# Gate and up of a SwiGLU network by seven block products in place of eight, with spills through DRAM

## The chip, the cores and the metric

The kernel runs on one core of a Trainium2 chip. Times are device microseconds of one execution. The version before was run three times: 1843.7 to 1844.92 us, median 1844.18. A separate profiled execution gives the trace that is read here. Engines go by the names of the profile: PE (TensorE, matrix products), DVE (VectorE), ACT (ScalarE), POOL (GpSimd), SP (SyncE, which here only issues DMA transfers). POOL issues DMA transfers as well.

## The reference

A decoder trunk of two layers on x of 1024 tokens by D = 1024 features, with a conditioning vector c. Each layer is a token mixer and a feed-forward network (FFN), each behind an RMSNorm, an affine step from c, and a gated residual add:

```python
def swiglu_ffn(h, w_gate, w_up, w_down):
    return (jax.nn.silu(h @ w_gate) * (h @ w_up)) @ w_down
```

The FFN has F = 2816 hidden columns, 22 tiles of 128. The mixer of layer 0 is a causal convolution module (pointwise to 2D, a gate, 31 taps per channel, LayerNorm, silu, pointwise to D). The mixer of layer 1 takes trailing means over 2, 4, 8 and 16 tokens, less the token itself, and maps them by four small matrices. A last RMSNorm ends the stack. All is float32.

## The kernel before

Features lie on the 128 partitions (eight tiles k or d of 128), tokens on the free axis, in two chunks A and B of 512. So one matmul is a 128 x 128 weight tile by 128 x 512 activations into one PSUM bank. There are six banks for products and two spare ones. Every product is made of three matmuls (`products`, L434): weight and activation are each split into a rounded part and the rest, and high by high, high by low, and low by high are summed. The activations are `hhi` and `hlo`, the weights a pair in one `w` tile.

`load_weight` (L419) makes a `w` tile of 128 x 1024: SP loads `raw`, ACT casts it into the high half and writes its negative into the low half, and POOL issues a second, accumulating load of the same weights onto it (`summed`). The other way, a subtraction on DVE or POOL (`either` picks by a table of prices), is used for a few.

The order on PE is the order of the program: a list of units, each with the weights that it takes, which `run_units` (L561) loads up to five tiles ahead. Work for the other engines that may run beside them (taps of the convolution, norms, pooling) is cut into tasks that `pace` steps forward between products by the price table; `need` finishes a task. Each engine keeps its own row of instructions in order, and a waiting row holds back all behind it.

`ffn` (L921) goes through one chunk's 22 tiles: `ffn_p1` (L883) makes gate and up of a tile, 24 matmuls each, and g = silu(gate) x up as a pair (ACT, DVE, ACT, then DVE or POOL); `ffn_p2` (L909) multiplies two g's by their rows of the down weights into eight tiles d, and DVE adds each, scaled, to x. The whole of x and both chunks' g stay in SBUF. The main order (L1173 to L1224) is: FFN of A in layer 0 with B's taps beside it; B's convolution output and norm three units before its end; FFN of B with A's pooling beside it; FFN of A in layer 1, with the last down units of B and B's pooling; FFN of B. So while one chunk's norm is under way on DVE, PE has products of the other chunk.

Of the kernel before, what the change touches and what calls it, by code (L numbers as in the profile page):

```python
# [9 lines left out]
F32 = mybir.dt.float32  # L10
# [6 lines left out]
P = 128  # L17
D = 1024
# [18 lines left out]
GROUP = 2  # L37
# [12 lines left out]
OUT_B = 3  # L50
LOAD = {"load": 4.0, "slow": 18.0, "next": 4.0, "dots": 4.0}
# [67 lines left out]
def trunk(ctx, tc, xT, c, vec, ada, adan, w1f, w1, wdg, w2, wgu, wdn, wpl, out):  # L119
# [12 lines left out]
    def matmul(out, lhsT, rhs, start, stop):  # L132
        n = out.shape[-1]
        clock["PE"] += n / 2400 * (1 if rhs.dtype == F32R else 4) + 0.0025
        last_mm[0] = nc.tensor.matmul(out, lhsT, rhs, start=start, stop=stop).ins.name  # L135
# [27 lines left out]
    slots = ctx.enter_context(tc.tile_pool(name="slots", bufs=2 * KT))  # L163
# [3 lines left out]
    ps = ctx.enter_context(tc.tile_pool(name="ps", bufs=BANKS, space=bass.MemoryType.PSUM))  # L167

# [74 lines left out]
    def slot(ch, name, dt=F32R):  # L243

        return slots.tile([P, ch.n], dt, tag=f"s{ch.i}", name=nm(name))
# [10 lines left out]

    def gslots(ch):

        pair = wpair(ch, "g", F32R)
        return pair[:, 0, : ch.n], pair[:, 1, WSLOT - ch.n :]  # L260
# [30 lines left out]
    xp = [[cst.tile([P, 2, ch.n], F32, name=f"x_{ch.i}_{k}") for k in range(KT // 2)] for ch in chunks]  # L291
    x = [[pairs[k // 2][:, k % 2] for k in range(KT)] for pairs in xp]
    for k in range(KT // 2):
        load_next(xp[0][k], xT[0, :, 2 * k : 2 * k + 2])
# [139 lines left out]
    def products(out, wt, k, act, first, last, o=0, n=None):  # L434

        wk = slice(k * P, (k + 1) * P)
        for i, (wp, a) in enumerate(((0, 0), (0, 1), (1, 0))):
            cols = act[a][:, o : o + n] if n else act[a]
            matmul(out, wt[:, wp, wk], cols, start=first and i == 0, stop=last and i == 2)
# [104 lines left out]
    def norm(ch, l, ffn, key, keep=False, squares=None):  # L544
        h = [(slot(ch, "hhi"), slot(ch, "hlo")) for _ in range(KT)]
# [15 lines left out]
    def run_units(cap, early):  # L561

        queue = [w for ws, _ in units for w in ws]
        loaded = list(early)
        del queue[: len(early)]
        used = [0]

        def ahead(free):
            while queue and len(loaded) + used[0] - free < cap:
                src = queue.pop(0)  # L570
                loaded.append(src() if callable(src) else load_weight(src, summed=True))
                if len(loaded) > 1:
                    break

        for ws, emit in units:
            def take():
                ahead(0)
                used[0] += 1
                return loaded.pop(0)
            emit(take)  # L580
            used[0] -= len(ws)
            ahead(0)
            pace()
# [58 lines left out]
    def split_u(p):  # L642

        u = st["u", 0, p][:, HALO - 2 : HALO - 2 + A.n]
        hi, lo = st["us", p] = [slot(A, name) for name in ("uhi", "ulo")]
        S_.copy(hi, u)
        either(A.n).tensor_tensor(lo, u, hi.bitcast(F32), op=SUB)
# [101 lines left out]
    def layer_norm_silu(ch):  # L749
# [26 lines left out]
        hv = [(slot(ch, "vhi"), slot(ch, "vlo")) for _ in range(KT)]  # L776
# [60 lines left out]
    def pool_mixed(ch, k):  # L837
# [20 lines left out]
        hi, lo = st["mx", ch.i, k] = slot(ch, "mxhi"), slot(ch, "mxlo")  # L858
# [4 lines left out]
    def pool_out(ch, l, pair):  # L863
        def emit(take):
            wt = take()
            for gi in range(2):
                g = pair * 2 + gi
                for m in range(2):
# [4 lines left out]
                    update(ch, d, b, gate_m, l)  # L873
                pace()
# [8 lines left out]
    def ffn_p1(ch, l, f, pick, first):  # L883
        def emit(take):
            h = st["h", ch.i]
            outs = [output(name, pick) for name in ("gate", "up")]
            if first:
                wts = [take(), take()]
                for k in range(KT):
                    for o, wt in zip(outs, wts):  # L890
                        products(o, wt, k, h[k], k == 0, k == KT - 1)
                    pace()
            else:
                for o in outs:
                    wt = take()
                    for k in range(KT):
                        products(o, wt, k, h[k], k == 0, k == KT - 1)
                        if k % 4 == 3:
                            pace()
            hi, lo = st["g", ch.i, f] = gslots(ch)  # L900

            t = window(ch.n, "gt") if ch.i == 0 and l == 0 and f >= NF - 2 else temp(ch.n)
            S_.activation(t, outs[0], AF.Silu)
            V_.tensor_tensor(t, t, outs[1], op=MUL)
            S_.copy(hi, t)
            either(ch.n).tensor_tensor(lo, t, hi.bitcast(F32), op=SUB)
        return emit, (wgu[l, f, 0], wgu[l, f, 1])

    def ffn_p2(ch, l, fs, pick):  # L909
        def emit(take):  # L910
            wd = [take() for _ in fs]
            gs = [st.pop(("g", ch.i, f)) for f in fs]
            for d in range(KT):
                b = output("dn", pick)
                for i, (g, wt) in enumerate(zip(gs, wd)):
                    products(b, wt, d, g, i == 0, i == len(gs) - 1)
                update(ch, d, b, gate_f, l)
                pace()
        return emit, tuple(wdn[l, f] for f in fs)

    def ffn(ch, l, pick, at_end=False):  # L921

        us, pend = [], None
        ends = [NF - n for n in range(0, NF, GROUP)][::-1]
        if NF % GROUP == 1:
            ends[0] += 1
        for f0, f1 in zip([0] + ends, ends):
            fs = list(range(f0, f1))
            for i, f in enumerate(fs):
                us.append(ffn_p1(ch, l, f, pick, l == 0 and f == 0))  # L930
                if i == (len(fs) - 1 if fs[-1] == NF - 1 else 0) and pend is not None:
                    us.append(pend)
            last = at_end and fs[-1] == NF - 1
            pend = ending(ch, l, fs) if last else ffn_p2(ch, l, fs, pick)
        us.append(pend)
        return us

    def ending(ch, l, fs):
# [27 lines left out]
        def emit(take):  # L966
            wd = [take() for _ in fs]
            gs = [st.pop(("g", ch.i, f)) for f in fs]
# [81 lines left out]
    h_a = st["h", 0] = [(slot(A, "hhi"), slot(A, "hlo")) for _ in range(KT)]  # L1050
# [100 lines left out]
    unit(lambda take: T.__setitem__("ada_f", ada_task(0, (4, 5), "dots", "slow")))  # L1151
    for p in rest[len(rest) - HOLD - HOLD_LN : len(rest) - HOLD]:
        conv_in((B, p))
    need("ln_a")
# [9 lines left out]
    for p in rest[len(rest) - HOLD :]:  # L1164
        conv_in((B, p))
    need("norm_a")
# [6 lines left out]
    taps(B, *range(KT))  # L1173
    put("ln_b", lambda: layer_norm_silu(B))
    fa = ffn(A, 0, False)
    for i, (e, ws) in enumerate(fa):
        if i == GROUP + 1:
            unit(lambda take: finish(T["ada_f"]))
            unit(lambda take: T.__setitem__(("ada", 1), ada_task(1, range(6))))
        if i == len(fa) - OUT_B:  # L1180
            need("ln_b")
            sq_b = Squares(B)
            conv_out(B, sq_b)
            unit(lambda take: T.__setitem__("norm_bf", Task(norm(B, 0, True, ("h", 1), squares=sq_b), True)))
        unit(e, *ws)
    need("norm_bf")
    unit(lambda take: stretch.__setitem__(0, 1.0))

# [6 lines left out]

    unit(lambda take: (lax.__setitem__(0, True), st.__setitem__("taps_done", True)))

    def with_pool(us, ch, at, out_at):

        for i, (e, ws) in enumerate(us):  # L1200
            if i == at:
                if ch.i == 0:
                    ada_need((1, 0), (1, 1), (1, 2))
                put(("pool", ch.i), lambda: pool(ch))
            if i == out_at:
                need(("pool", ch.i))
                for q in range(2):
                    pool_out(ch, 1, q)
                if ch.i == 0:
                    ada_need((1, 3), (1, 4), (1, 5))  # L1210
                put(("nf", ch.i), lambda: norm(ch, 1, True, ("hn", ch.i), True))
            unit(e, *ws)
        need(("nf", ch.i))
        unit(lambda take: st.__setitem__(("h", ch.i), st["hn", ch.i]))


    fb_, fa_, last = ffn(B, 0, True), ffn(A, 1, True), ffn(B, 1, True, at_end=True)
    with_pool(fb_[:-1], A, 3, 14)
    with_pool(fa_[:1] + fb_[-1:] + fa_[1:-1], B, 5, 17)
    for i, (e, ws) in enumerate(last[:1] + fa_[-1:] + last[1:]):  # L1220
        if i == 3:
            put("final_a", lambda: final(A))
        unit(e, *ws)
# [53 lines left out]
```

## Time and profile before

| what | value |
|---|---|
| median of three runs | 1844.18 us |
| span of the profiled execution | 1848.1 us |
| PE busy | 1805.3 us, 8106 matmuls |
| DVE, ACT, POOL busy | 985.4, 971.0, 622.3 us |
| DMA | 388.61 MB, mean 210 GB/s |
| granted PE clock in the FFN stages | 0.99 to 1.00 |

The page gives busy time by engine, then 40 slices of the span, DMA queues, the chain of work that ended last, and groups of instructions. A group's row reads: line, engine, operation, output<-inputs by the program's names (buffer numbers left out), shapes, count, then busy time, mean ns of one, and idle time of its engine just before with what ended it. L113 and L135 are the two helpers that record every operation, so the tiles' names tell them apart. A waits row reads: total us, times, longest. A timeline row reads: start, length, engine. DMA rows end with the median us from issue to landing.

### The profile page before, as it was taken

To read this page: it belongs to the slowest core of one execution; us is meant where nothing else is said; L and a number is where in the kernel's file an instruction comes from. 1 tells how busy PE (TensorE), PEld (TensorE's weight loads), DVE (VectorE), ACT (ScalarE), POOL (GpSimd) and SP (SyncE) were. 2 spreads that over 40 slices of the span, in tenths; PEclk is the share of its full clock that TensorE was granted. 3 is DMA by queue.
4 is the path that set the end of the run, shared out by engine and by line. 5 is a ranking of instruction groups with operands and counts; after the bars stand their busy time and mean duration, and the time that the engine had idled before them with its cause. 6 is when DMAs were issued, how large, how long until landed. Compare 5 with 4: busy or idle time off the path is not lost.

```text
span 1848.1 us, 21822 instructions
## 1 busy us (share of the span) xinstructions
PE 1805.3 (98%) x8106; PEld 1483.8 (80%) x8106; DVE 985.4 (53%) x1522; ACT 971.0 (53%) x1244; POOL 622.3 (34%) x662
## 2 busy tenths in 40 slices
PE   6999999999999999999999999999999999999997
PEld 4777787888888888778888888888888888888886
DVE  7889857988884245576622233734432233323225
ACT  3666666767756364454544435644544454444443
POOL 3587534887834112263111112511111111111111
PEclk9999999999999999999999999999999999999998
DMA  6959888988978888989887888878878879788782
GB/s 262 292 159 236 202 237 246 255 212 217 237 194 224 220 221 199 278 257 268 229 199 176 211 182 201 186 180 211 190 173 207 198 178 247 176 208 195 181 197 69
DMA packets 108573, 388.61 MB, mean 210 GB/s; under 512 B 11825, under 2 KB 14001, under 8 KB 108466
## 3 DMA queue, kind: packets, MB, share of 16 engines
q0 software_dynamic: 44352, 161.50, 47.6%
q1 hardware_dynamic: 63024, 224.65, 35.0%
q8 instruction: 64, 1.05, 0.2%
q10 hardware_dynamic: 1090, 1.05, 0.2%
q14 instruction: 43, 0.35, 0.1%
HBM read 382.96 MB, written 4.19 MB: 209 GB/s over the span
## 4 chain that ended last, share of the span: by engine, by line
PE 84%; DVE 10%; DMA 4%; issue 1%; ACT 0%; SPq 0%; DVEq 0%
PE gate L135 24%; PE up L135 24%; PE dn L135 24%; PE y L135 6%; DVE ca L113 4%; DMA adaw<-in_ada_dram 3%; PE first L135 2%; PE a L135 2%; PE g L135 2%; DVE acc L113 1%; DVE adaw L113 1%; DVE t L113 1%; DVE hlo L113 1%; DVE x L113 1%; DMA adaw<-in_adan_dram 1%
## 5 line engine op out<-in xcount | busy, mean ns | idle before, releaser
L113 ACT CAST w<-raw 128x1024 fp32r<-128x1024 f32 x318 | 332.4, 1045 | 496.4 <-issue 286.5
L135 PE MATMUL dn<-g,w 128*128 128x512 f32 (+1 forms) x2160 | 490.5, 386 | 0.7 <-DVE t L113 0.7
L135 PEld LDWEIGHTS dn<-g,w 128*128 128x128 f32 x2160 | 399.7, 189 | 82.5 <-DVE t L113 1.5
L135 PE MATMUL gate<-hhi,w 128*128 128x512 f32 x1408 | 451.5, 390 | 1.9 <-DVE x L113 1.9
L135 PE MATMUL up<-hhi,w 128*128 128x512 f32 x1408 | 451.0, 390 | 0.0
L428 POOL DMA_DIRECT2D w<-in_wgu_dram x176 | 154.3, 877 | 744.0 <-ACT w L113 733.0
L113 ACT ACTIVATE w<-raw 128x1024 fp32r<-128x1024 f32 x308 | 325.2, 1056 | 0.0
L113 DVE SCALAR_TENSOR_TENSOR x<-dn,gains,x 128x512 f32<-128x512 f32 (+1 forms) x360 | 261.7, 735 | 110.7 <-PE dn L135 107.5
L135 PEld LDWEIGHTS gate<-hhi,w 128*128 128x128 f32 x1408 | 265.0, 188 | 57.4 <-DVE x L113 2.3
L113 DVE TENSOR_TENSOR t<-t,up 128x512 f32<-128x512 f32 x86 | 59.0, 686 | 469.7 <-PE up L135 447.4
L135 PEld LDWEIGHTS up<-hhi,w 128*128 128x128 f32 x1408 | 264.4, 188 | 54.7
L135 PE MATMUL gate<-hlo,w 128*128 128x512 f32 x704 | 274.8, 390 | 2.7 <-DVE hlo L113 2.7
L135 PE MATMUL up<-hlo,w 128*128 128x512 f32 x704 | 273.9, 389 | 0.0
L113 POOL TENSOR_TENSOR pa<-pa,pr 128x512 f32<-128x512 f32 x158 | 227.2, 1546 | 18.5 <-ACT pr L113 15.8
L113 DVE SCALAR_TENSOR_TENSOR ca<-u,vecs,ca 128x512 f32<-128x512 f32 x247 | 171.2, 746 | 0.2
L135 PEld LDWEIGHTS gate<-hlo,w 128*128 128x128 f32 x704 | 132.6, 188 | 31.4 <-DVE hlo L113 4.0
L135 PEld LDWEIGHTS up<-hlo,w 128*128 128x128 f32 x704 | 132.2, 188 | 27.1
L428 POOL DMA_DIRECT2D w<-in_wdn_dram x88 | 78.5, 892 | 217.3 <-ACT w L113 215.5
L113 DVE SCALAR_TENSOR_TENSOR adaw<-adaw,cact 128x1024 f32<-128x1024 f32 x80 | 120.2, 1503 | 58.7 <-DMA adaw<-in_ada_dram 58.5
L113 ACT ACTIVATE t<-gate 128x512 f32<-128x512 f32 x86 | 51.0, 593 | 149.1 <-PE gate L135 147.3
L113 ACT ACTIVATE pr<-u,vecs 128x512 f32<-128x512 f32 x158 | 106.7, 714 | 27.4 <-DVE u L113 9.5
L113 DVE TENSOR_TENSOR g<-t,g 128x512 fp32r<-128x512 f32 x66 | 55.0, 833 | 62.5 <-ACT g L113 62.5
(143 smaller groups left out, 1601.3 us busy)
## 6 DMA issues: line engine op xcount, KB each, us to landing
raw<-in_wgu_dram SPq DMA_DIRECT2D x176, 512.0 KB, 7.5
w<-in_wgu_dram POOLq DMA_DIRECT2D x176, 512.0 KB, 8.1
raw<-in_wdn_dram SPq DMA_DIRECT2D x88, 512.0 KB, 5.3
w<-in_wdn_dram POOLq DMA_DIRECT2D x88, 512.0 KB, 9.2
adaw<-in_ada_dram SPq DMA_DIRECT2D x64, 512.0 KB, 7.5
raw<-in_w_dram SPq DMA_DIRECT2D x36, 512.0 KB, 6.3
w<-in_w_dram POOLq DMA_DIRECT2D x34, 512.0 KB, 8.5
adaw<-in_ada_dram SPq DMA_DIRECT2D x8, 1024.0 KB, 6.6
```

What stands on the lines that cost most here:

```text
L113: self.last = self.order(getattr(self.eng, name)(out, *args, **kw))
L135: last_mm[0] = nc.tensor.matmul(out, lhsT, rhs, start=start, stop=stop).ins.name
L428: order(nc.gpsimd.dma_start(low if len(src.shape) == 2 else low.rearrange("p (a b) -> p a b", a=src.shape[1]), src, accum_op=ADD))
```

## The change

Gate and up of a layer are one product of weights by activations. The change cuts it in blocks: F tiles in pairs (even and odd, 11 pairs), the contraction in two halves of four tiles k, and the tokens in A and B. Eight block products for each of gate and up become seven, of the kind that Strassen's and Winograd's schemes use: two of them (`head`) give A's even tile from A alone; five (`joint`) use sums of weight quarters and sums of activations of both chunks and give B's even, B's odd and A's odd tile. A block product is four tiles k by three matmuls; `head` and `joint` make it for gate and for up, in two banks.

* `head(l, fp)`: the first half's product is kept, also in DRAM (`rd`); the second is added, and g of A's even tile goes to DRAM (`gd`).
* `joint(l, fp)`: parts t1 (banks e), t2 (banks a), b22 (e again), T3 (a again), T4 (a again). After each bank DVE makes a sum out of it, before the next part adds to that bank. The weights come from four raw quarters, one accumulating load and three adds, each result split by a cast and a subtraction. Every g goes to DRAM.
* `combinations(l)` makes the activations t1, t2, b22, T3 after B's norm; `last_combination` makes T4.
* `downs` fetches g from DRAM in groups of four tiles and does four tiles d at a time; every second weight is split by subtraction rather than by an accumulating load.
* x of a chunk is written to DRAM and read back (`x_out`, `x_in`) where its slots hold activations; the slots are cut otherwise (a ring of four 128 x 2 x 512 blocks `u0` for r, g, s2 and fetched g).
* Order: all 11 heads of layer 0; downs of A's even tiles, with B's convolution output after the second group and the combinations started after the third; all joints; downs of A's odd tiles; downs of B, with A's pooling; heads of layer 1 with B's pooling and the combinations started after the eighth; joints; downs of A, downs of B. B's taps start before A's LayerNorm has ended.

```diff
-GROUP = 2
+NP = NF // 2
+GROUP = 4
-LOAD = {"load": 4.0, "slow": 18.0, "next": 4.0, "dots": 4.0}
+LOAD = {"load": 4.0, "slow": 6.0, "next": 4.0, "dots": 4.0}
...
+    def gated(l, i, f, g, u, sign, tag):
+
+        S_.activation(g, g, AF.Silu, scale=sign)
+        V_.scalar_tensor_tensor(g, u, sign, g, op0=MUL, op1=MUL)
+        both = block(tag, "g")
+        split(g, both)
+        sync.dma_start(gd[l][i][f], both.bitcast(F32))
...
+        def second(take):
+            wt, h, bs, r = take(), st["h", 0], two_banks("p2"), st.pop(("r", fp))
+            for o, b in enumerate(bs):
+                for j in range(4):
+                    products(b, wt, 4 * o + j, h[4 + j], j == 0, j == 3)
+                pace()
+            g, u = temp(512), temp(512)
+            V_.tensor_tensor(g, bs[0], r[:, 0], op=ADD)
+            V_.tensor_tensor(u, bs[1], r[:, 1], op=ADD)
+            gated(l, 0, 2 * fp, g, u, 1.0, "u0")
...
+        def s1():
+            for i in (2, 3, 0, 1):
+                w[i] = quarter(l, fp, i, "u1")
+            order(nc.gpsimd.dma_start(w[0], wgu[l, fp, 2], accum_op=ADD))
+            either(D).tensor_tensor(w[2], w[2], w[3], op=ADD)
+            return combined(w[2])
+
+        def s2():
+            w[4] = block("u0", "s2", F32).rearrange("p a b -> p (a b)")
+            either(D).tensor_tensor(w[4], w[0], w[3], op=ADD)
+            return combined(w[4])
+
+        def s4():
+            either(D).tensor_tensor(w[1], w[1], w[4], op=ADD)
+            return combined(w[1])
...
+        unit(part("t1", "e", 0, after5, False, load), s1)
+        unit(part("t2", "a", 0, after6, False), s2)
+        unit(part("b22", "e", 0, ended("r2", 1, 2 * fp, 1.0), True), s4)
+        unit(part("T3", "a", 0, ended("r15", 1, 2 * fp + 1, -1.0), True), s3)
+        unit(part("T4", "a", 0, ended("r1", 0, 2 * fp + 1, -1.0), True), a22)
...
+        for j in range(4):
+            t = ts[j] = temp(512)
+            e = either(512)
+            e.tensor_tensor(t, f(a[j][0]), hb[j][:, 0], op=SUB)
+            e.tensor_tensor(t, t, f(a[j][1]), op=ADD)
+            parts("t1", j, t, "x1")
+            yield
...
+    downs(A, 0, even, "u0", {1: conv_b, 2: lambda: start_combinations(0)})
+    unit(lambda take: stretch.__setitem__(0, 1.0))
+    unit(lambda take: T.__setitem__(("ada", 1), ada_task(1, range(6))))
+    all_joint(0, fetch(A, 0, odd[:GROUP], "h0"))
```

How the rows move is seen at three places. First PE, at B's FFN norm in layer 0. Before, `var` and `rstd` (the norm's two small products) stand among A's gate and up products:

```order
L135 MATMUL gate_945_5706<-hlo_421_2501,w_906_5529 128x512
L135 MATMUL gate_945_5706<-hhi_420_2500,w_906_5529 128x512
L135 MATMUL var_947_5732<-ones_91,acc_890_5439 128x1 [waits DVE_49]
L135 MATMUL var_947_5732<-ones_91,acc_890_5439 128x1 x3
L135 MATMUL up_946_5707<-hhi_406_2486,w_912_5572 128x512 [waits Activation_49]
```

Now the last even downs end ahead of them, and what follows is the first joint product, which takes t1:

```order
L135 MATMUL dn_792_4794<-g_701_4260,w_772_4664 128x512 x3
L135 MATMUL dn_793_4795<-g_701_4260,w_772_4664 128x512 x3
L135 MATMUL var_803_4858<-ones_205,acc_746_4501 128x1 [waits DVE_49]
L135 MATMUL var_803_4858<-ones_205,acc_746_4501 128x1 x3
L135 MATMUL rstd_805_4876<-ident_209,col_804_4864 128x128 [waits DVE_49]
L135 MATMUL rstd_805_4876<-ident_209,col_804_4864 128x128 x3
L135 MATMUL e_842_5006<-t1_808_4902,w_780_4709 128x512 [waits Activation_49]
L135 MATMUL e_842_5006<-t1_808_4902,w_780_4709 128x512 [waits Pool_49]
```

No product stands between the norm and its use any more. Second POOL, at the same place. Before, its row holds accumulating loads (L428) and one subtraction of g:

```order
L428 DMA w_927_5683<-in_wdn_dram 128x1024 [waits DMASW4_49,PE_49,Activation_49]
L428 DMA w_961_5819<-in_wdn_dram 128x1024 [waits DMASW4_49,PE_49,Activation_49]
L428 DMA w_963_5825<-in_wgu_dram 128x1024 [waits DMASW5_49,PE_49,Activation_49]
L113 TENSOR_TENSOR g_958_5811<-gt_959_5812,g_958_5811 128x512 [waits Activation_49]
L428 DMA w_973_5895<-in_wgu_dram 128x1024 [waits DMASW6_49,PE_49,Activation_49]
```

Now (`hb` is B's normed input, `h` A's, `raw` and `s2` are weight quarters and their sums):

```order
L443 DMA w_772_4664<-in_wdn_dram 128x1024 [waits DMASW5_49,PE_49,Activation_49]
L113 TENSOR_TENSOR w_796_4843<-raw_777_4701,w_796_4843 128x1024 [waits DMASW1_49,Activation_49]
L966 DMA raw_848_5040<-in_wgu_dram 128x1024 [waits DMAHW6_49,DVE_49]
L113 TENSOR_TENSOR s2_856_5082<-raw_848_5040,raw_847_5038 128x1024 [waits DMAHW5_49,DMASW2_49]
L113 TENSOR_TENSOR raw_849_5042<-raw_849_5042,s2_856_5082 128x1024 [waits DMAHW0_49,Pool_49]
L113 TENSOR_TENSOR t_807_4899<-h_429_2723,hb_797_4846 128x512 [waits Activation_49]
L113 TENSOR_TENSOR b22_819_4939<-hb_797_4846,b22_819_4939 128x512 [waits Activation_49]
L113 TENSOR_TENSOR t_809_4905<-h_430_2724,hb_798_4847 128x512 [waits Activation_49]
```

The steps of t1 stand behind the second joint's weights: a load, and two sums that wait for it. Third SP, between the heads and the even downs of layer 0. Before, its row at that part of the FFN is loads of weights:

```order
L422 DMA raw_644_3867<-in_wgu_dram 128x1024 [waits DMAHW3_49,Activation_49]
L422 DMA raw_648_3875<-in_wdn_dram 128x1024 [waits DMAHW5_49,DMAHW0_49,Activation_49]
L145 DMA adaw_633_3807<-in_ada_dram 128x1024 [waits DVE_49]
L422 DMA raw_657_3961<-in_wdn_dram 128x1024 [waits DMAHW6_49,Activation_49]
L422 DMA raw_661_3969<-in_wgu_dram 128x1024 [waits DMAHW7_49,Activation_49]
```

Now writes of g (`gd`), which wait for POOL's subtraction, and fetches of it stand among them:

```order
L145 DMA g_663_4010<-gd_0_0_2_91 128x1024 [waits DMAHW7_49,DMAHW3_49]
L145 DMA g_664_4012<-gd_0_0_4_93 128x1024 [waits DMAHW4_49,DVE_49]
L437 DMA raw_689_4162<-in_wdn_dram 128x1024 [waits DMAHW1_49,Activation_49]
L145 DMA gd_0_0_20_109<-g_659_3998 128x1024 [waits DMAHW2_49,Pool_49]
L145 DMA g_665_4014<-gd_0_0_6_95 128x1024 [waits DMAHW2_49]
L145 DMA g_675_4092<-gd_0_0_8_97 128x1024 [waits DMAHW6_49,PE_49]
```

The fourth fetch of the first group, g_665, stands behind the write of the last head's g_659.

More of the change, by code (lines that the diff above doesn't have):

```diff
@@ L438, in products @@
             cols = act[a][:, o : o + n] if n else act[a]
-            matmul(out, wt[:, wp, wk], cols, start=first and i == 0, stop=last and i == 2)
+            matmul(out, wt[:, wp, wk], cols, start=first and i == 0, stop=last and i == 2, more=more)
     def rsqrt(v, y, t):
@@ L909, in ffn_p2, with split @@
[L909 to L936, printed above, removed]
+    def split(t, dst):
+        S_.copy(dst[:, 0], t)
+        either(t.shape[-1]).tensor_tensor(dst[:, 1], t, dst[:, 0].bitcast(F32), op=SUB)
```

322 lines of the change are left out of this document (243 added, 79 removed).

## The prediction

> **What bounds the kernel now.** The page comes first: its head, the share of each engine, and the chain that ended last.
>
> ```profile
> span 1848.1 us, 21822 instructions
> PE 1805.3 (98%) x8106; PEld 1483.8 (80%) x8106; DVE 985.4 (53%) x1522; ACT 971.0 (53%) x1244; POOL 622.3 (34%) x662
> PE 84%; DVE 10%; DMA 4%; issue 1%; ACT 0%; SPq 0%; DVEq 0%
> ```
>
> TensorE is busy 98% of the span. The table by stage (busy time of each engine, then granted clock, DMA share, GB/s) says where the rest lies:
>
> ```profile
> 0.00:303.00 303.00, 281.02 (x1304) 220.85 (x1305) 246.03 (x388) 181.84 (x246) 160.60 (x173) 0.99 0.82 239
> 303.00:692.00 389.00, 386.29 (x1715) 318.92 (x1715) 272.76 (x393) 250.68 (x330) 215.82 (x191) 1.00 0.87 219
> 692.00:1284.00 592.00, 586.88 (x2596) 485.26 (x2595) 280.88 (x429) 289.93 (x359) 154.15 (x192) 0.99 0.85 213
> 1284.00:1809.00 525.00, 525.00 (x2334) 435.41 (x2333) 160.60 (x243) 234.84 (x277) 86.17 (x98) 1.00 0.83 195
> ```
>
> From 303 us, where the feed-forward network (FFN) of chunk A starts, to 1809, PE idles 2.71 + 5.12 + 0.00 = 7.8 us in 1506. So a matmul that goes is worth its whole time there, and any new wait of PE costs its whole length. The chain in order of time gives the price of one, at a full granted clock:
>
> ```profile
> 317.71 5.45 PE gate L135 x24
> 323.17 5.44 PE up L135 x24
> ```
>
> 5.44 / 24 = 0.2267 us per matmul (the 390 ns in the groups below overlap). The groups give the counts:
>
> ```profile
> L135 PE MATMUL gate<-hhi,w 128*128 128x512 f32 x1408 | 451.5, 390 | 1.9 <-DVE x L113 1.9
> L135 PE MATMUL up<-hhi,w 128*128 128x512 f32 x1408 | 451.0, 390 | 0.0
> ...
> L135 PE MATMUL gate<-hlo,w 128*128 128x512 f32 x704 | 274.8, 390 | 2.7 <-DVE hlo L113 2.7
> L135 PE MATMUL up<-hlo,w 128*128 128x512 f32 x704 | 273.9, 389 | 0.0
> ```
>
> 2 x (1408 + 704) = 4224 matmuls of gate and up. What PE can wait for is visible in its list of waits, which is short because the old order hides each norm behind another chunk's products:
>
> ```profile
> PE rstd L135 <- DVE col L113: 13.0, 4, 4.6
> PE var L135 <- DVE acc L113: 7.8, 2, 7.2
> ```
>
> **The gain.** Per pair of F tiles, eight block products become seven, two in `head` and five in `joint`, each of 4 tiles k x 3 matmuls for gate and as many for up, 24: 11 pairs x 2 layers x 7 x 24 = 3696 in place of 4224. 528 x 0.2267 = **-119.7 us**. The down products stay 2160. I also let the old 7.8 us of idle go, since every wait of the new order is priced anew below: **-127.5** together.
>
> **The waits it adds.** The new order can no longer lay A's products over B's norms: `joint` needs both chunks' inputs. Each term is PE time from the last product that can run to the first that waits. Prices of small steps:
>
> ```profile
> L113 DVE SCALAR_TENSOR_TENSOR x<-dn,gains,x 128x512 f32<-128x512 f32 x344 | 254.3, 747 | 109.3 <-PE dn L135 106.2
> L113 DVE TENSOR_TENSOR t<-t,up 128x512 f32<-128x512 f32 x86 | 59.0, 686 | 469.7 <-PE up L135 447.4 <-PE dn L135 11.5 <-ACT t L113 10.8
> L113 DVE TENSOR_TENSOR acc<-acc,t 128x512 f32<-128x512 f32 x77 | 53.2, 691 | 30.5 <-ACT t L113 27.6
> L113 DVE SCALAR_TENSOR_TENSOR hlo<-t,mod,hhi 128x512 fp32r<-128x512 f32 x48 | 43.7, 929 | 2.3 <-ACT hhi L113 2.1
> L113 DVE TENSOR_TENSOR w<-raw,w 128x1024 fp32r<-128x1024 f32 x2 | 2.4, 1220 | 0.0
> L113 DVE SCALAR_TENSOR_TENSOR adaw<-adaw,cact 128x1024 f32<-128x1024 f32 x80 | 120.2, 1503 | 58.7 <-DMA adaw<-in_ada_dram 58.5
> L113 POOL TENSOR_TENSOR pa<-pa,pr 128x512 f32<-128x512 f32 x158 | 227.2, 1546 | 18.5 <-ACT pr L113 15.8
> L113 POOL TENSOR_TENSOR g<-t,g 128x512 fp32r<-128x512 f32 x20 | 32.3, 1616 | 1.7 <-ACT g L113 1.6
> ...
> L113 POOL TENSOR_TENSOR w<-raw,w 128x1024 fp32r<-128x1024 f32 x8 | 22.8, 2852 | 30.1 <-ACT w L113 20.3 <-DVE mod L113 9.8
> ```
>
> ```profile
> 295.78 0.95 PE L135 MATMUL var<-ones,acc 128*128 128x1 f32 x8
> ...
> 300.57 2.06 DVE L113 SCALAR_TENSOR_TENSOR t<-x,gains,rstd 128x512 f32<-128x512 f32 x3 [1.42 <-PE rstd L135]
> ```
>
> The last two, from the timeline, price one norm's inner step: 4.8 us from the sum of squares on PE to the first use of its root.
>
> ```profile
> raw<-in_wgu_dram SPq DMA_DIRECT2D x176, 512.0 KB, 7.5
> w<-in_wgu_dram POOLq DMA_DIRECT2D x176, 512.0 KB, 8.1
> raw<-in_wdn_dram SPq DMA_DIRECT2D x88, 512.0 KB, 5.3
> w<-in_wdn_dram POOLq DMA_DIRECT2D x88, 512.0 KB, 9.2
> ...
> out_dram<-x SPq DMA_DIRECT2D x12, 256.0 KB, 8.6
> ...
> out_dram<-x ACTq DMA_DIRECT2D x4, 256.0 KB, 2.3
> ```
>
> 1. *Layer 0, heads to even downs.* g waits in DRAM, and the fourth fetch stands in SP's queue behind the write of the last head's g. After the last head: two adds, silu, product, cast and subtraction, about 4.6 us; a write never seen in this size, 2.3 to 8.6 by the two output rows, taken as 6; a fetch of 512 KB, 5.3. That is 16 us, while three tiles of products cover 36 x 0.2267 = 8.2. Eight us, and six more since the conv taps of B now share POOL with the heads (61 `pa` x 1.55 = 94 us, ten g's x 1.6, a dozen issues: about as long as the heads' own 120 us): **14** (6 to 25).
> 2. *LayerNorm of conv B*, after the second group of even downs. Eight centrings near 0.69, seven adds (0.691) and three more updates (0.747), 12.6 us of DVE, stand before the variance; 24 matmuls (5.4) cover part, and the centrings can begin a little before the last product: 6.5. The root: 4.8. Then `v` needs a silu, a cast and a POOL subtraction per tile, and POOL's queue holds a weight add that waits for its loads: some 13 before y runs freely. **24** (17 to 30).
> 3. *Combinations of layer 0.* Nothing of PE is left after the last even down (at V): variance, root, modulated B, then t1. With free engines e would start at about V + 8 (root 4.8, the first b and its ACT step 1.4, three short steps). But POOL's t1 steps stand behind an accumulating load of weights (9.2 at most by its rows), which itself waits for a buffer that a weight subtraction frees at V + 4, and behind two adds that wait for it, 2.85 each: 4 + 9 + 5.7 = V + 19. Nine POOL steps of 1.6 follow: V + 33. DVE has one add of weights ahead of its root. **33** (24 to 40).
> 4. *Combinations of layer 1.* Heads go on beside them; but some 25 DVE steps of the combinations stand before the two adds that free the banks of the ninth head's second half, due 14.7 us after the root, reached after some 25: **11** (4 to 14).
> 5. *FFN norm of A in layer 1* now stands alone before the heads, as no B down is kept back: root 4.8, and a first `hlo` with its step ahead (929 + 741 ns), updates between: **8** (5 to 10).
> 6. *22 joints* of 120 matmuls, 27.2 us each. In layer 1 a joint has 19 DVE steps: six of 1024 columns at 1.22 and thirteen near 0.7, 16.5 us; POOL has two weight subtractions, three g's and an issue, 11.4. T4 adds to the bank that DVE has just read after T3, with 2.7 us to do it. I take 0.3 us a joint: **6** (0 to 25).
> 7. *Downs in groups of four*: half the weights come by accumulating load, half by subtraction; the second is ready about when due. **5** (0 to 15).
> 8. *LayerNorm and norm of A* with B's taps started before them: **3** (0 to 6).
>
> Bytes are no term: by the rows of the order SP gains 178 transfers of 512 KB and 44 of 256 KB (spills, their fetches, fewer weights) and POOL loses 174 accumulating loads of 512 KB, so 388.6 becomes some 402 MB, and a joint moves under 240 GB/s where the page has slices up to 292:
>
> ```profile
> GB/s 262 292 159 236 202 237 246 255 212 217 237 194 224 220 221 199 278 257 268 229 199 176 211 182 201 186 180 211 190 173 207 198 178 247 176 208 195 181 197 69
> DMA packets 108573, 388.61 MB, mean 210 GB/s; under 512 B 11825, under 2 KB 14001, under 8 KB 108466
> ```
>
> Sum of the waits: 14 + 24 + 33 + 11 + 8 + 6 + 5 + 3 = 104; all low ends 56, all high ends 165. The profiled execution becomes 1848.1 - 127.5 + 104 = 1824.6 (1776.6 to 1885.6). The median of the runs, 1844.18, lies 3.9 below the profile, so **1821** on the runs' scale (1773 to 1882).
>
> **Rivals.**
>
> *Waits at their low ends.* Terms 1, 2 and 3 rest on what stands ahead in POOL's and SP's queues; the engines may reach those rows earlier than I place them, since DVE and POOL were busy only 53% and 34%. Halfway between the low ends and my values (80) the time is 1797, at the low ends 1773; I put this case at 1785. Against it: in the stage of the heads, POOL carries about its whole length.
>
> *Slower: the joints become the bound, because DVE and POOL hold each other off.* The timeline has a pair of steps that shows it, and the tile view of g on DVE its spread (minimum, median, maximum in ns):
>
> ```profile
> 375.47 3.05 POOL L113 TENSOR_TENSOR pa<-pa,pr 128x512 f32<-128x512 f32 x2
> 375.55 1.80 DVE L113 TENSOR_TENSOR g<-t,g 128x512 fp32r<-128x512 f32 x1
> ...
> L113 DVE TENSOR_TENSOR g<-t,g x66: 682/693/4293, 331.0 to 1811.8; 128x512 fp32r<-128x512 f32 x66
> L113 DVE SCALAR_TENSOR_TENSOR ca<-u,vecs,ca x247: 739/746/757, 78.6 to 520.3; 128x512 f32<-128x512 f32 x124
> ```
>
> A DVE step that reads two tiles from SBUF and begins under a POOL step took 1.80 instead of 0.69 us; `ca`, with one operand in PSUM, never varied under the same POOL steps. [...] As a mechanism of this kernel, from the rows: a joint puts nine such DVE steps (six wide, three gated products) beside 10.5 us of POOL in 27.2: four in ten meet one, with about 1.1 us left of it, so 4 us more: 20.5 us in layer 1; in layer 0 three `adaw` steps of 1.5 bring 25, beside waits for PE and ACT. It decides once a joint is over by 24 / 22 = 1.1 us beyond my 0.3. With 3.8 us in layer 0 and 1.3 in layer 1, it is 11 x 5.1 = 56 us in place of the 6: 1871. For it: DVE's margin in layer 0 is 2 us in 27. Against: the banks let a joint's last adds run into the next one, and the wide weight steps have some 10 us of lead.
>
> *Break-even*, in which the waits come out near 120 to 130: 1837 to 1848.
>
> **How the numbers follow.** My forecast 0.43; low ends 0.17; slower by the joints or by several waits at their high ends 0.31; the rest, near break-even, 0.09, of which 0.06 within 0.2% (3.7 us, about what a measurement of this kernel tells from no change) and 0.03 just faster. So faster 0.43 + 0.17 + 0.03 = 0.63, same 0.06, slower 0.31. The range 1785 to 1878 leaves out half of the low case (0.08) and the far part of the slower one (0.12). The likeliest case alone: 1803 to 1837.
>
> **What would show it.** PE busy near 1805.3 - 119.7 = 1686 us at the same clock; a pair of joints at 54 us on PE, and more if the slower rival holds, with waits of PE on DVE at e and a; gaps of PE named e <- POOL or DVE once, of about 33 us, at layer 0; y <- ACT or POOL near 24; dn <- a DMA of g at the first even group. If those gaps are under half, the low case holds. The prediction is wrong in its basis if a matmul costs other than 0.2267 or the granted clock falls in the joints.

## The result and the profile after

The changed kernel takes 1933.08 us (median of 4 runs, 1931.03 to 1936.32) against 1844.55 us for the kernel before: 1.0473 times as long, 95% interval 1.0451 to 1.0495. The forecast was 1821 us in a range from 1785 to 1878.

The head of its page: span, busy time, and the granted PE clock in 40 slices (tenths of full speed).

```profile
span 1934.5 us, 21602 instructions
PE 1737.4 (90%) x7578; PEld 1409.1 (73%) x7578; DVE 1326.4 (69%) x1768; ACT 830.1 (43%) x1118; POOL 830.5 (43%) x666
...
PEclk9999898998796899999999999997899999999998
```

The 528 matmuls are gone (8106 to 7578). But PE is busy 1737.4 us, 52 more than the 1805.3 - 119.7 = 1685.6 that the prediction counted on, and idle 197 us in place of 43. The clock row, at 9 nearly throughout before, drops in slices where PE waits. The rows below are stages. Their columns are the window, its length, the busy time (and count) of PE, PEld, DVE, ACT and POOL, the granted clock, the DMA share and GB/s. The stages are, in order: the heads of layer 0; the even downs with B's convolution output; the combinations and joints of layer 0; the start of layer 1's joints; the rest of them.

```profile
330.00:449.40 119.40, 114.97 (x495) 93.83 (x495) 115.07 (x139) 87.96 (x131) 104.93 (x81) 0.99 0.74 216
449.40:590.60 141.20, 115.78 (x483) 93.20 (x482) 72.37 (x106) 63.31 (x86) 45.26 (x37) 0.89 0.73 210
590.60:960.00 369.40, 303.92 (x1250) 244.72 (x1250) 272.03 (x304) 106.74 (x142) 174.58 (x100) 0.89 0.57 178
...
1330.00:1371.00 41.00, 23.60 (x98) 18.84 (x96) 38.78 (x36) 16.35 (x25) 28.91 (x18) 0.79 0.30 102
1371.00:1660.00 289.00, 279.48 (x1225) 230.89 (x1224) 169.10 (x202) 94.29 (x117) 110.57 (x65) 0.98 0.57 175
```

In the third row PE is idle for 65 us, in the last for only 10, nearly all of it at its start. What PE waits for (total, times, longest):

```profile
PE var L135 <- DVE acc L113: 36.5, 7, 11.6
PE e L135 <- DVE t L113: 28.2, 4, 15.5
PE p L135 <- DVE t L113: 21.3, 5, 17.4
PE rstd L135 <- DVE col L113: 20.5, 7, 6.0
PE a L135 <- DVE t L113: 20.4, 9, 4.6
PE e L135 <- ACT t L113: 15.6, 1, 15.6
...
PE dn L135 <- DMA g<-gd: 11.4, 3, 9.8
```

Over the whole span DVE ends 139 us of the waits that are listed for PE, DMA 27 and ACT 21, so it is mostly DVE that PE waits for. (In this trace's names p is a head's bank, e and a are a joint's banks, h and T are activations, and t is the temporary tile in which DVE makes activations and sums alike.)

Each stage's loss is the time from its first product to the first of the next stage, less 0.2267 us for each product of 512 columns and 0.1 us for each small product of a norm (eight in a row take 0.81). Term 8 is the 18.3 us by which the first head starts later than A's first gate product did before (321.3 against 303.0 us, with 971 products of 512 columns ahead of it in both), and 8.2 us lost within the heads. Term 7 ends at 1842.8 us; the tail behind it is left out.

| the prediction's term | predicted us | measured us |
|---|---|---|
| 1 heads to even downs, first groups | 14 | 15 |
| 2 LayerNorm of conv B | 24 | 20 |
| 3 combinations of layer 0, to the first T3 | 33 | 52 |
| 4 combinations of layer 1, heads and first joint | 11 | 43 |
| 5 norm of A in layer 1, and the heads behind it | 8 | 10 |
| 6 joints after that: layer 0, layer 1 | 6 together | 36, 0 |
| 7 downs | 5 | 17 |
| 8 norm of A in layer 0 and the heads behind it | 3 | 27 |
| sum | 104 | 220 |

The spans give 1934.5 - 1848.1 + 127.5 = 214 for the same sum; of the 6 us between them, 3.5 are slow products that the kernel before had too (shown further down). For instance the joints of layer 0, from the first T3 at 659.28 to the last T4's end at 977.97: 318.7 - 1248 x 0.2267 = 36. The gain itself came as reckoned: the joints of layer 1, from 1388.3 to 1671.3, took 283.0 us for the same 1248.

### The profile page after: what moved, and what is told of

Read it like the earlier page. It is cut to its first block, busy times and chain, and to the rows that moved or that the text cites. A ratio compares the mean times of both kernels' runs of the same rounds, so it can differ in the third digit from the quotient of the medians.

```text
span 1934.5 us, 21602 instructions
## 1 busy us (share of the span) xinstructions
PE 1737.4 (90%) x7578; PEld 1409.1 (73%) x7578; DVE 1326.4 (69%) x1768; ACT 830.1 (43%) x1118; POOL 830.5 (43%) x666
## 4 chain that ended last, share of the span: by engine, by line
PE 40%; DVE 15%; DMA 11%; issue 8%; POOL 3%; ACT 3%; DVEq 0%; POOLq 0%; ACTq 0%; SPq 0%
PE dn L135 17%; PE a L135 11%; PE e L135 7%; DMA w<-in_wdn_dram 4%; DVE t L113 4%; DMA raw<-in_wgu_dram 4%; PE p L135 3%; PE y L135 2%; DVE w L113 1%; DMA raw<-in_wdn_dram 1%; DVE r L113 1%; ACT w L113 1%; DVE hb L113 1%; DVE win L113 1%; DVE acc L113 1%
## 5 line engine op out<-in xcount | busy, mean ns | idle before, releaser
L135 PE MATMUL a<-T,w 128*128 128x512 f32 x1056 | 256.3, 402 | 22.2 <-DVE t L113 20.4
L135 PE MATMUL p<-h,w 128*128 128x512 f32 x1056 | 250.4, 398 | 27.2 <-DVE t L113 21.3
L135 PEld LDWEIGHTS a<-T,w 128*128 128x128 f32 x1056 | 204.5, 195 | 70.7 <-issue 25.9
L135 PEld LDWEIGHTS p<-h,w 128*128 128x128 f32 x1056 | 201.5, 192 | 74.0 <-DVE t L113 23.8
L113 DVE SCALAR_TENSOR_TENSOR x<-dn,gains,x 128x512 f32<-128x512 f32 (+1 forms) x200 | 136.6, 726 | 169.6 <-PE dn L135 169.5
L113 DVE TENSOR_TENSOR w<-raw,w 128x1024 fp32r<-128x1024 f32 x120 | 176.3, 1469 | 53.6 <-ACT w L113 53.4
L135 PE MATMUL e<-b,w 128*128 128x512 f32 x528 | 128.0, 399 | 26.4 <-DVE t L113 26.4
L135 PE MATMUL e<-t,w 128*128 128x512 f32 x528 | 127.6, 398 | 20.5 <-ACT t L113 15.6
L135 PE MATMUL a<-t,w 128*128 128x512 f32 x528 | 123.2, 389 | 0.0
L113 ACT ACTIVATE w<-raw 128x1024 fp32r<-128x1024 f32 x112 | 118.2, 1056 | 0.0
```

Source lines behind the costliest of these rows:

```text
L113: self.last = self.order(getattr(self.eng, name)(out, *args, **kw))
```

## Experiments

All are edits of the changed kernel, unless another is named. **Theory A** is that DVE's row does it: a step that stands for something, or steps put ahead, hold back the reads that free PE's banks. **Theory B** is that DVE and POOL block each other on their SBUF reads (in the kernel before, a DVE step with two SBUF inputs took 1.80 us under a POOL step, against a median of 0.69). **Theory C** is the traffic of the spills.

What one joint of layer 0 looks like on DVE (timeline):

```profile
924.10 0.69 DVE L113 TENSOR_TENSOR r<-a,r 128x512 f32<-128x512 f32 x1 [0.56 <-PE a L135]
933.24 1.22 DVE L113 TENSOR_TENSOR s<-raw,raw 128x1024 f32<-128x1024 f32 x1 [8.46 <-DMA raw<-in_wgu_dram]
934.38 0.68 DVE L113 TENSOR_TENSOR r<-a,r 128x512 f32<-128x512 f32 x1
934.98 3.08 DVE L113 SCALAR_TENSOR_TENSOR adaw<-adaw,cact 128x1024 f32<-128x1024 f32 x1
...
941.89 0.68 DVE L113 TENSOR_TENSOR t<-a,t 128x512 f32<-128x512 f32 x1
942.50 1.69 DVE L113 SCALAR_TENSOR_TENSOR adaw<-adaw,cact 128x1024 f32<-128x1024 f32 x1
```

and PE beside it:

```profile
942.72 8.21 PE L135 MATMUL a<-T,w 128*128 128x512 f32 x24 [4.58 <-DVE t L113]
```

DVE stands 8.46 us for an accumulating load of weights, takes a late read, then an `adaw` step (layer 1's modulation), and reaches `t<-a,t`, which T4 waits for, 4.6 us too late. (That `adaw` step took 3.08 us beside a step of POOL, where most take 1.2, so what theory B names lengthens the delay.) In layer 1 DVE stands as long, but without `adaw` it is back in time:

```profile
1519.44 1.23 DVE L113 TENSOR_TENSOR s<-raw,raw 128x1024 f32<-128x1024 f32 x1 [7.86 <-DMA raw<-in_wgu_dram]
1520.59 0.68 DVE L113 TENSOR_TENSOR t<-e,r 128x512 f32<-128x512 f32 x1
...
1529.93 0.69 DVE L113 TENSOR_TENSOR t<-a,t 128x512 f32<-128x512 f32 x1 [2.03 <-PE a L135]
```

**e1_no_ada.** No `adaw` in the joints (leaves out layer 1's modulation; layer 0's is copied).

```diff
-    unit(lambda take: T.__setitem__(("ada", 1), ada_task(1, range(6))))
+    unit(ada_copy)
...
```

> Leaves out the 48 dot products (adaw) that make layer 1's modulation; layer 1 uses layer 0's instead. Theory A (DVE's row: in the joints of layer 0 DVE stands some 8 us for an accumulating load of weights, and then two adaw steps push the reads that free T4's banks past their time): the joints of layer 0 run like those of layer 1, PE loses under 6 us there in place of 36, so about 1900 us. Theory B (DVE and POOL block each other on their reads of SBUF, and that is what makes DVE late): the blocking stays, only 48 short steps go, about 1920. Theory C (traffic of the spills): 25 of 402 MB go, 1925 or more.

Measured: 1890.42 us, 43 less than the changed kernel.

**e2_sum_on_engine.**

```diff
-            order(nc.gpsimd.dma_start(w[0], wgu[l, fp, 2], accum_op=ADD))
+            either(D).tensor_tensor(w[0], w[0], w[2], op=ADD)
```

> The sum of two weight quarters is made by an add on DVE or POOL in place of the accumulating load; adaw stays. Theory A: DVE has no 8 us to stand for, catches up in spite of adaw, and the T4 waits of layer 0 go: about 1903 us. Theory B: one more wide step with two SBUF inputs in each joint, no gain, 1930 to 1945. Theory C: 22 loads fewer, 1930.

Measured: 1905.38 us, 28 less. The joints of layer 0 from the first T3 to the downs, by stage tables: the changed kernel, with its layer 1 below,

```profile
659.30:978.00 318.70, 296.51 (x1250) 240.51 (x1249) 219.20 (x255) 93.60 (x118) 135.71 (x79) 0.96 0.67 213
1388.30:1671.30 283.00, 283.00 (x1250) 234.19 (x1249) 158.36 (x194) 95.60 (x118) 105.60 (x62) 1.00 0.60 186
```

without `adaw`,

```profile
662.30:945.20 282.90, 282.90 (x1250) 234.23 (x1248) 157.73 (x195) 96.35 (x118) 102.83 (x61) 1.00 0.58 180
```

and with the sum on an engine and `adaw` in place:

```profile
656.20:945.00 288.80, 284.27 (x1250) 233.87 (x1249) 243.69 (x264) 93.78 (x118) 137.39 (x70) 1.00 0.65 217
```

Either removal cures the joints: 318.7 to 282.9 or 288.8, with PE without a pause in the first. So it takes both, the stand for the load and the `adaw` steps. With the sum on an engine DVE does more (244 us in 289), and POOL as much, and still the joints hardly wait: blocking between DVE and POOL (theory B) alone costs no more than the 5.9 us that stay, and traffic (217 GB/s there, more than the 213 of the changed kernel) nothing that shows.

**e4_ada_later.** The `adaw` steps after the joints of layer 0.

```diff
-    unit(lambda take: T.__setitem__(("ada", 1), ada_task(1, range(6))))
     all_joint(0, fetch(A, 0, odd[:GROUP], "h0"))
+    unit(lambda take: T.__setitem__(("ada", 1), ada_task(1, range(6), "next")))
```

> The same 48 adaw steps begin only after the joints of layer 0, beside the down products, where DVE is busy 60% of the time. Theory A: the joints of layer 0 lose under 6 us in place of 36, and the downs of B pay up to 8 for adaw: 1900 to 1910 us. Theory B: the joints keep most of their loss: 1920. Theory C: no change, 1930.

Measured: 1937.71 us, no gain. Joints, then downs (odd tiles of A, and B):

```profile
656.80:940.10 283.30, 283.12 (x1249) 234.14 (x1248) 158.07 (x196) 95.90 (x118) 104.24 (x62) 1.00 0.58 180
940.10:1177.50 237.40, 209.65 (x874) 168.32 (x872) 167.72 (x249) 76.24 (x90) 65.16 (x81) 0.94 0.91 299
```

The joints are cured as in e1, as theory A said. But the downs take 237.4 us in place of 209.1 (978.0 to 1187.1 in the changed kernel), and the next stage 8 more. PE waits there for DVE's updates of x (9.7 us in the whole run) and for A's pooled tiles (6.8). That these stand behind the modulation's steps is argued from the order and not shown, and how the rest divides was not taken apart. That price was put at 8 and was 36: moved from the joints to the downs, `adaw` cost as much there.

**e3_comb_dve.** All steps of the combinations on DVE.

```diff
-            e = either(512)
+            e = V_
...
-            split(t, both)
+            split(t, both, V_)
```

> All additions and subtractions of the combinations on DVE, none on POOL. Theory B: beside POOL a DVE step of 512 columns takes 1.75 us and a POOL step 1.71, so two steps take 1.75; alone DVE takes 0.68 a step, so the combinations end sooner: PE's waits at the first joint of each layer fall by 15 to 25 us together, 1908 to 1918. Theory A alone (a step takes what it takes): DVE's row gets some 20 steps more in each layer, 5 to 15 us slower, 1938 to 1948.

Measured: 1931.08 us. The steps take as long as theory B said. In the changed kernel, beside POOL (DVE, then POOL):

```profile
611.81 1.75 DVE L113 TENSOR_TENSOR t<-h,hb 128x512 f32<-128x512 f32 x1
613.48 1.75 DVE L113 TENSOR_TENSOR b<-hb,b 128x512 fp32r<-128x512 f32 x1
```

```profile
611.30 3.38 POOL L113 TENSOR_TENSOR t<-t,h 128x512 f32<-128x512 f32 x2
614.65 1.71 POOL L113 TENSOR_TENSOR b<-hb,b 128x512 fp32r<-128x512 f32 x1
```

and with POOL left out:

```profile
607.25 0.68 DVE L113 TENSOR_TENSOR t<-h,hb 128x512 f32<-128x512 f32 x1
607.85 0.68 DVE L113 TENSOR_TENSOR b<-hb,b 128x512 fp32r<-128x512 f32 x1
```

Side by side, the two engines made two steps in some 1.7 us; DVE alone made two in 1.28 (608.45 to 609.73 in that trace). That it is the SBUF reads rests on the prediction's rows of `ca`; no run tested it apart. As a whole the kernel took as long as before the edit, within the spread of the runs. Up to the first T3 of layer 0 it saved 10 us and in layer 1 4, less than the 15 to 25 expected, and later stages gave nearly all back: 3 in the joints of layer 0, 3 in the downs, 4 in the joints of layer 1.

**e5_t4_later.** In the changed kernel the task for T4 stands ahead of the reads of e and a. DVE, at the first joint of layer 0:

```profile
637.29 6.16 DVE L113 SCALAR_TENSOR_TENSOR t<-t 128x512 f32<-128x512 f32 x3
643.37 0.68 DVE L113 TENSOR_TENSOR r<-a,r 128x512 f32<-128x512 f32 x1
...
649.20 0.68 DVE L113 TENSOR_TENSOR t<-e,r 128x512 f32<-128x512 f32 x1
```

The product b22 adds to the bank that `t<-e,r` reads: it waited 15.5 us, to 649.93. The edit starts the task after the second part:

```diff
-        unit(lambda take: T.__setitem__("last", Task(last_combination(l), True)))
...
         unit(part("t2", "a", 0, after6, False), s2)
+        if start:
+            unit(lambda take: T_.__setitem__("last", Task(last_combination(l), True)))
...
```

> The task that makes T4's activations starts after the second part of a layer's first joint, so its steps stand behind the reads of banks e and a in DVE's row and no longer ahead of them. Theory A (place in DVE's row): the wait at b22, 15.5 us in layer 0 and 9.5 in layer 1, goes, and at most 2 to 5 us come back at T4: 1912 to 1920. Rival D (DVE has too much to do there, in whatever order): the wait moves to T4 in full, 1930 to 1935.

Measured: 1932.86 us. The waits of e on DVE fell from 28.2 to 8.5 us, those of a rose from 20.4 to 33.9, and the weights of the downs came later:

```profile
PE a L135 <- DVE t L113: 33.9, 10, 8.4
...
PE e L135 <- DVE t L113: 8.5, 3, 3.0
```

The first T3 came 17 us earlier in layer 0, counted from V (the start of the norm's sums behind the last even down, 589.65 us in the changed kernel), and 6 in layer 1, counted from the first e; the joints behind it took 8 and 10 longer. Rival D holds: a better place in the row only moves the wait, since DVE has the same work to do before T4.

**e6_heads_over** puts the last two heads of layer 0 (96 products, 21.8 us) beside the combinations. Their two even tiles go down with the odd ones, and t2 takes slots of x of A, which is written out and read back.

```diff
...
-    downs(A, 0, even, "u0", {1: conv_b, 2: lambda: start_combinations(0)})
+    downs(A, 0, even[:9], "u0", {1: conv_b})
+    unit(lambda take: x_out(A))
+    start_combinations(0)
+    for fp in range(9, NP):
+        head(0, fp)
...
```

> The last two heads of layer 0 (98 matmuls short of 22 us) stand after B's convolution output, beside the combinations, and their two even tiles go down with the odd ones. Rival E (the combinations of layer 0 only lack products to lie beside): of 15.6 + 3 us waited for t1 some 15 go, 1915 to 1920. Theory A: the heads' own adds stand behind the combinations' steps on DVE, as in layer 1, so p waits in place of e, with the wait for B's LayerNorm longer besides: 1925 to 1940.

Measured: 1931.61 us. The longest wait for the first e is now 23.7 us, though heads lay beside the combinations: from V to the first e it takes 45.4 us in place of 24.6, longer by about what the two heads take. Cover alone, rival E, isn't it.

**e7_taps_late** restores the old start of B's taps.

```diff
-    taps(B, *some, *rest[: len(rest) - HOLD - HOLD_LN])
...
+    taps(B, *range(KT))
     put("ln_b", lambda: layer_norm_silu(B))
```

> B's taps start only when the FFN of A starts, as before the change. Theory A: the sums of squares and A's norm are no longer behind taps in DVE's row, so the heads start some 18 us earlier, at 303 in place of 321; the taps then last into the even downs and B's LayerNorm waits for them by about as much, since heads and even downs give them 163 us where the old order gave 220: 1925 to 1945. Rival: the taps find room and the 18 us stay, 1915.

Measured: 1955.92 us, 23 more. The heads start at 300.3 us in place of 321.3, as expected, and PE then waits 36 us for B's LayerNorm:

```profile
PE mean L135 <- DVE acc L113: 39.2, 2, 36.0
```

The heads lose 8 us among themselves as in the changed kernel. So the 18 us by which the heads start late are the price of an early start of the taps, and the late start costs more; the 8 within the heads are not the taps'.

**e8_gaps** tests another suspicion, theory F: that PE runs slowly for a while after a wait. It is the kernel before, with the same products and chains of DVE steps of set lengths ahead of them.

```diff
+            if ch.i == 0 and l == 1 and 1 < f < 20:
+                gap((0, 3, 8, 14, 25, 50)[f % 6])
...
```

> The kernel before, with 18 waits put ahead of gate products of A in layer 1: a small product, a chain of 1, 4, 9, 15, 26 or 51 small steps of DVE on its result, and a small product on that (three of each length; the numbers are not used). Theory F (PE restarts slowly after a wait): waits up to about 2 us cost themselves alone, longer ones 1.5 to 2.8 us more in the products behind them, the same for 3 us and for 11. Against it: the products behind any wait run at 0.2267 us, and the slow ones of the changed kernel are slow for another reason, such as their operands. The whole: 3 x (1.6 + 2.3 + 3.3 + 4.5 + 6.7 + 11.7) = 90 us of waits, and 12 x 2.2 = 26 more by theory F.

Measured, in one run: a span of 1968.8 us, 88.7 of it in the waits. Products behind a wait of 12.48 us and of 0.80:

```profile
1357.39 0.59 PE L135 MATMUL gap<-gapcol,ident 128*128 128x1 f32 x2 [12.48 <-DVE gapcol L113]
1357.84 0.77 PE L135 MATMUL gate<-hhi,w 128*128 128x512 f32 x1
1358.41 0.63 PE L135 MATMUL gate<-hlo,w 128*128 128x512 f32 x1
1358.84 1.05 PE L135 MATMUL gate<-hhi,w 128*128 128x512 f32 x2
1359.69 0.63 PE L135 MATMUL gate<-hlo,w 128*128 128x512 f32 x1
...
1371.91 0.38 PE L135 MATMUL gap<-gapcol,ident 128*128 128x1 f32 x2 [0.80 <-DVE gapcol L113]
1372.15 0.48 PE L135 MATMUL gate<-hhi,w 128*128 128x512 f32 x1
1372.47 0.39 PE L135 MATMUL gate<-hlo,w 128*128 128x512 f32 x1
```

After the long wait products start 0.43 us apart (1358.41 to 1358.84), after the short one 0.23; in the changed kernel, behind its wait of 17.40 us, the granted clock is 0.50 from 1347.7 to 1350.7 us and 1.00 from 1352 to 1355. Over the 48 products behind a wait, less the 0.4 us that the short waits show too, waits of 0.80 to 1.36 us cost nothing more. Of three waits of 2.31 us two cost 1.6 more and one nothing. Waits of 3.43 us cost 1.6 more, 5.4 to 12.5 us 1.9 to 2.6, and 16.7 us 2.9. Theory F holds, with an edge near 2 us that is not sharp: it is the wait and not the operands. In the changed kernel the same excess, 1.5 to 2.8 us, stands behind each of its 15 or so longer waits (the shortest of them 2.16 us; waits of 2.07 and 2.11 show 0.2 and 0.45), some 35 of the 52 us by which PE is busier.

**e9_three_edits**: e2, e3 and e5 together.

> The sum of quarters on an engine, the combinations on DVE alone and T4's activations after the second part, together. Alone they gave -28, -2 and 0 us. If what undid the last two was DVE being full in the joints of layer 0 (theory A with D), they count now, since the standing for the accumulating load is gone: joints of both layers lose under 8 us, and the waits up to the first T3 fall by 10 + 12 us in layer 0 and 8 in layer 1: 1880 to 1890. If not, the sum of the three, 1903.

Measured: 1896.12 us, 37 less than the changed kernel, between the two expectations. The stretch from V to the first T3 of layer 0 fell by 26 us, the one from layer 1's first head to its first T3 by 15. But the joints of layer 0 took 302.6 us from there, 14 more than with e2 alone, and those of layer 1 13 more, most of it in one wait of 7.8 us at the first T4 and the slow products behind it.

**e10_three_first**: e9, and the even downs in groups of 3, 4, 4.

```diff
-        return [fs[i : i + GROUP] for i in range(0, len(fs), GROUP)]
+        n = len(fs) % GROUP if fs[0] == 0 and fs[1] == 2 else 0
+        return ([fs[:n]] if n else []) + [fs[i : i + GROUP] for i in range(n, len(fs), GROUP)]
```

> As the one before, with the even downs of layer 0 in groups of 3, 4, 4 in place of 4, 4, 3, so that the first group needs no fetch behind the write of the last head's g. If the wait of 10 + 1.4 us at the first even group is that fetch, as the prediction had it, it falls to under 3 and the restart of 2 us goes with it: 10 us less than the kernel before it. If PE waits there for any fetch, or for POOL and DVE behind the taps, no change.

Measured: 1897.18 us, and 12.3 us of wait at the first even group, as before. Already the first three fetches go out late, at 453.7 us in the changed kernel, behind weights that wait in SP's row. The fourth is not the cause: it went out at 467.5 us, when PE had been at the even downs for 8 us, and cost one wait of 1.4. Term 1 had the right size for a reason that does not hold; that was luck.

**e11_paced**: e10, and the combinations of layer 1 not all at once.

```diff
-        unit(lambda take: T.__setitem__("comb", Task(combinations(l, st["sq"]), True)))
+        unit(lambda take: T.__setitem__("comb", Task(combinations(l, st["sq"]), not l, 0)))
```

> As the one before, with the combinations of layer 1 stepped by the price table among the heads in place of all at once, so that the adds which free the heads' banks are not behind them in DVE's row. Theory A: p's wait of 17 us goes, with its restart, and not more than 6 come back at the first joint: 12 to 18 us less. Rival D: the wait moves to e, no change.

Measured: 1900.83 us. The heads' wait went, from 16.0 to 2.1 us at most, and came back in the first joint, at b22, as one of 21.0:

```profile
PE e L135 <- DVE t L113: 26.8, 4, 21.0
...
PE p L135 <- DVE t L113: 4.3, 4, 2.1
```

**e12_heads_paced**: e9, with the combinations of both layers paced, and the two heads of e6.

> The first of these four with the combinations of both layers paced, and the last two heads of layer 0 beside them. With DVE's steps short and spread, the heads can cover the combinations of layer 0: e's wait falls by 15 us more than in the first of the four, at the price of up to 10 at B's LayerNorm; with the 15 of layer 1 some 15 to 20 less than the first. By rival D (DVE has no room for it) no more than the 15 of layer 1.

Measured: 1894.14 us, the lowest median of a version that computes the whole, but only 2 less than e9, which is within the spread of the runs, and still 1.0275 (1.024 to 1.0311) times the kernel before. In all these runs, where DVE has to make the combinations in a stretch, cover and order move the wait and do not remove it.

## Why the prediction was wrong

**The gain held.** 528 matmuls at 0.2267 us, and joints that run at that pace in layer 1, without a pause.

**The waits came to 220 us in place of 104** (214 by the spans), and four steps made most of the difference.

* *Term 6, "I take 0.3 us a joint"*: 36 us in layer 0. The step added up DVE's busy time against 27.2 us, and left out the place where DVE stands in its row for the accumulating load. Eight us of standing and 16.5 of work still fit, as layer 1 shows; with `adaw` they don't. e1 and e2 show both parts. The slower rival had the stage and the size (3.8 us a joint in layer 0; measured 3.3) but by blocking between DVE and POOL alone, which e2 rules out as the main cause there, and it gave layer 1 1.3 where nothing was lost.
* *Terms 3 and 4, the combinations*: 52 and 43 in place of 33 and 11. The step for t1 came out right, by its path too: POOL's steps for it ran from V + 17 to V + 34, forecast as V + 19 to V + 33. The first e started 614.25 - 589.65 = 24.6 us after V, and its products ended at 628.9. What it left out came after: the steps for T4 that follow on DVE, with PE at b22 behind them, 15.5 us in layer 0 and 9.5 in layer 1. In layer 1 the wait of the heads' banks was 17.4 us in place of 11, and one of 9.4 us for B's sum of squares came ahead of it. e5, e9 and e11 show that it is DVE's work there, lengthened beside POOL's (1.75 us a step in place of 0.68, e3), and not only the order.
* *Term 8, 3 us*: 27. Of these 18 are the taps now ahead of A's sums on DVE (e7); what the 8 within the heads come from was not tested. The prediction named the overlap and gave it no working.
* *A price that no term had*: PE's slow restart, mostly 1.5 to 2.9 us behind each wait over about 2 us (e8), some 35 us in all, contained in the measured column. The prediction made a fall of the clock in the joints a condition and set no price for it, though the trace of the kernel before has it at two places in the FFN stages. Behind the wait of 15.48 us at b22 the granted clock was 0.50 (650 to 653 us), and in e8 products started 0.43 us apart in place of 0.23. Not every wait near 2 us was enough: one of 1.86 us in the kernel before cost 1.8, one of 2.16 in the changed kernel 1.7, one of 2.11 only 0.45.

The kernel before, behind a wait of 2.56 us (a timeline row, then two stage rows, whose third and eighth entries are PE and the granted clock):

```profile
784.77 1.26 PE L135 MATMUL rstd<-ident,col 128*128 128x128 f32 x8 [2.56 <-DVE col L113]
```

```profile
786.30:788.80 2.50, 2.50 (x7) 1.95 (x6) 0.00 (x0) 0.59 (x2) 2.17 (x2) 0.50 1.05 302
790.00:795.00 5.00, 5.00 (x24) 4.12 (x23) 4.82 (x8) 2.05 (x3) 1.44 (x2) 1.00 1.05 311
```

Just behind the wait the clock is 0.50 and the products start 0.43 us apart, 1.7 us lost in all; a wait of 1.86 us at 832.22 cost 1.8 in the same way. Averaged over stages of 300 to 600 us this disappears: the stage table has 0.99 to 1.00.

Terms 2 and 5 came within 4 us, and term 1 by its size. Term 7, the downs, is 17 in place of 5: PE waited some 11 us there for weights, and slow products followed the longest of these waits (4.3 us). Traffic was no term; e2 bears that out for the joints alone.

What stays open is how the 52 us of term 3 divide between the lengthening of DVE's steps beside POOL and DVE's bare work: e3 took 10 away, and no run made the combinations without two-input steps.

## What to carry to other kernels

When work is saved on the engine that bounds the kernel, price each new dependence by the row of the engine that serves it: a step that stands for a DMA, and every step ahead of the one that frees a bank, counts even if that engine has time to spare on average (here DVE was busy 69% of the span and stood 8.46 us for one load). Look at the granted clock just behind a wait and not only over a stage: in this kernel most waits of PE over some 2 us cost about 2 us beyond themselves. Where a reordering only moves a wait, as e5, e6 and e11 did here, look for the engine that is short of time in that stretch: it is its work that has to shrink.

## What the hardware showed beyond that

DVE and POOL, each with steps of two SBUF inputs, took 1.75 and 1.71 us a step of 512 columns side by side, where DVE alone took 0.68 (changed kernel and e3); the kernel's price table for `either` shares work out between them as if both ran at once. A wide DVE step of `adaw`, 1.22 us in the median, took 3.08 beside POOL.
